# Element-wise steps of the first half moved from GpSimd to VectorE, and the first norm's gains moved from the weights into the tokens

## The chip, the core and the metric

The kernel runs on one core of a Trainium2 chip. The core has five engines that work in parallel and meet at semaphores: TensorE (PE, matrix products; PEld is its weight load), VectorE (DVE), ScalarE (ACT), GpSimd (POOL) and SyncE (SP, which here only issues transfers). Each engine takes its instructions in one fixed order. The metric is the device time of one execution in microseconds (us). Lower is better.

## The reference, cut to what matters

One decoder layer for 2048 tokens of width 1024, all in float32. Only the first half (up to the output projection) is touched by the change:

```
h     = rmsnorm(x, norm1_g)                        # gains g of 1024 channels
proj  = h @ w_in                                   # 1024 -> 3*512 (attention) + 4*512 (HGRN)
# attention: three dilated branches per head, each gives o_b and lse_b
w     = softmax(lse_1, lse_4, lse_16);  o_attn = sum_b w_b * o_b
y_attn = rmsnorm(o_attn, attn_norm_g)
# HGRN2: gated recurrence, chunk by chunk
log_f = log(lb + (1-lb)*sigmoid(f_raw));  key = (1-lb)*sigmoid(-f_raw)
o_h   = rmsnorm(hgrn2(...), hgrn_norm_g);  y_hgrn = o_h * silu(gate)
x     = x + concat(y_attn, y_hgrn) @ w_out
x     = x + hier_moe(rmsnorm(x, norm2_g))          # 32 experts, top 2: not touched
out   = rmsnorm(x, norm_f_g)
```

## The kernel before, in words

The program has three stages. The first, up to about 1150 us, computes the projections, the attention and the HGRN heads; the second the output projection and the routing; the third, from about 1400 us, streams the experts' weights.

**Splitting into halves.** The large products of the first stage run as three float16 products of a high and a low part. `x_events` normalises each 128-token tile (line 226), turns it on PE (243) and splits it on ACT and DVE (246, 247). The projection weights come in pieces of 128 columns (`w_raw`): a transfer, a multiplication by the norm's gains on GpSimd (260), the sum of squares on ACT (`w_norm`, 291), a power-of-two scale (`w_scale`, `power`), and the split on ACT and DVE (`w_split`, 287, 288). The output weights go the same way in `b_weights` (GpSimd at 897).

**Pairs.** The first stage goes through four pairs of heads. For each there are projections of values (`v_tile`, PE at 386 to 388, cleared from PSUM by ACT at 393 and DVE at 394), of queries and keys (`qk_chunk`), and of the HGRN inputs (`h_tile`, PE at 567 to 569); 48 attention blocks; and four HGRN steps of 512 tokens each (`quad_steps`).

**Attention.** A block's scores (436) get bias and row maximum on DVE (440), the scaled maximum (447), the exponential on ACT (453), a split in halves on ACT and DVE (455, 456), a transposing transfer (458), and the product with the values (471, 473). The third branch is followed by `combine`: weights of the three branches from their maxima and sums (511 to 525 on DVE, 516 on ACT), then the weighted sum. Before, branch 0 is weighted on DVE and branches 1 and 2 on GpSimd (529), which also adds these two (531); DVE adds the rest (532).

**HGRN.** `gates` makes the forget gate and the key out of the projection: exponentials and logarithms on ACT (595 to 597, 601), products on DVE (598, 609) and three on GpSimd (599, 600, 602). The cumulative sum on PE (615) waits for the gate. `outputs` ends with a product on GpSimd (707).

**What sets the order.** PE's order is written out beforehand: a planner (`Runner`) strings the steps of all streams together by estimated costs and due times (`quad_steps`, for instance, allows 14,000 ns between gates and decays). The other engines' orders come out of a scheduler that follows that list with priorities, so that they shift when work moves from one engine to another.

Of the kernel before, what the change touches and what calls it, by code (L numbers as in the profile page):

```python
# [21 lines left out]
DM = 1024  # L22
# [142 lines left out]
class Layer:  # L165
# [34 lines left out]
    def x_events(self, xp, sp):  # L200
# [13 lines left out]
        def scaled(n):  # L214
# [8 lines left out]
            return rs  # L223

        def normed(n):
            nc.vector.tensor_scalar(X[n], X[n], scaled(n), None, op0=OP.mult)

        def step(n):
            if n == 0:
                for i in range(6):  # L230
                    load(i)
                for i in range(2):
                    normed(i)
# [18 lines left out]
    def w_raw(self, col, own=True):  # L252
        nc = self.nc
        if own and self.rawpool is not None:
            raw = self.rawpool.tile([128, KT, 128], F32, name="wraw0", bufs=3)
            nc.scalar.dma_start(raw, self.aps['w_in'][0, :, col:col + 128].rearrange("(t p) c -> p t c", p=128))
        else:
            raw = self.wpool.tile([128, KT, 128], F32, name="wraw", bufs=2)
            nc.sync.dma_start(raw, self.aps['w_in'][0, :, col:col + 128].rearrange("(t p) c -> p t c", p=128))
        nc.gpsimd.tensor_tensor(raw, raw, self.g1[:, :, None].to_broadcast([128, KT, 128]), op=OP.mult)  # L260
        return raw
# [31 lines left out]
    def w_steps(self, W, col, name, first):  # L293
# [7 lines left out]
        def split():  # L301
            w = W[name]
            w['sc'] = self.w_scale(w['ssp'], 1, "sc_" + name)
            self.w_split(w['raw'], w['sc'], w['wh'], w['wl'])
        a = Step(norm, 0, first)
        return [a, Step(split, 110, [(a, 10000)])]

    def h_weight_steps(self, p, W, first):
# [9 lines left out]
        def scale():  # L318
            nc = self.nc
            sc = W['sc'] = self.w_scale(W['ssp'], 4, "sc_h")  # L320
            inv = W['inv'] = self.wsm.tile([128, 2], F32, name="hinv")
            nc.vector.tensor_scalar(inv[:, 0:1], sc[:, 1:2], 1.0 / XSC, None, op0=OP.mult)
            nc.vector.tensor_scalar(inv[:, 1:2], sc[:, 1:2], -1.0 / XSC, None, op0=OP.mult)

# [173 lines left out]
    def combine(self, p, blk, rows, D):  # L498
# [14 lines left out]
        w = sm.tile([128, 3, 2, 2], F32, name="w")  # L513
        for b in range(3):
            nc.vector.tensor_sub(w[:, b], mn, nm[b])
        nc.scalar.activation(w, w, AF.Exp)
        den = sm.tile([128, 2, 2], F32, name="den")
        t = sm.tile([128, 3, 2, 2], F32, name="dent")
        for b in range(3):
            nc.vector.tensor_mul(t[:, b], w[:, b], s[b])  # L520
        nc.vector.tensor_add(den, t[:, 0], t[:, 1])
# [5 lines left out]
        for b in range(3):  # L527
            eng = nc.vector if b == 0 else nc.gpsimd
            eng.tensor_tensor(o[b], o[b], w[:, b, :, :, None].to_broadcast([128, 2, 2, 64]), op=OP.mult)
        eng = nc.gpsimd if 1 else nc.vector  # L530
        eng.tensor_tensor(o[1], o[1], o[2], op=OP.add)
        (nc.gpsimd if 1 > 1 else nc.vector).tensor_tensor(o[0], o[0], o[1], op=OP.add)
        dst = self.mix[512 * n:512 * n + 512, 128 * p:128 * p + 128].rearrange("(i r) c -> i r c", r=4)[:, r:r + 2, :]
# [47 lines left out]
    def quad_steps(self, p, q, H, ready):  # L581
# [4 lines left out]
        def gates():  # L586
# [11 lines left out]
            nc.vector.tensor_mul(key, key, f)  # L598
            nc.gpsimd.tensor_tensor(f, f, oml, op=OP.mult)
            nc.gpsimd.tensor_tensor(f, f, lb, op=OP.add)  # L600
            nc.scalar.activation(f, f, AF.Ln)
            nc.gpsimd.tensor_tensor(key, key, oml, op=OP.mult)

# [80 lines left out]
        def outputs():  # L684
# [3 lines left out]
            for i in range(4):  # L688
# [4 lines left out]
                for h in range(2):  # L693
# [12 lines left out]
                                    rs[:, :, None].to_broadcast([128, 8, 64]), op=OP.mult)  # L706
            nc.gpsimd.tensor_tensor(y, y, hq[:, :, 128:256], op=OP.mult)
            nc.sync.dma_start(self.mix[q * 512:q * 512 + 512, 512 + 128 * p:640 + 128 * p]
# [10 lines left out]
    def phase_a(self, ctx, pairs=range(NPAIR)):  # L719
# [10 lines left out]
        with pools:  # L730
# [9 lines left out]
            self.vp = pool("vp", 2)  # L740
            self.g1 = apool.tile([128, KT], F32, name="g1")
            nc.scalar.dma_start(self.g1, self.aps['norm1_g'][0].rearrange("(t p) -> p t", p=128))
            self.Sp = apool.tile([128, 8, 128], F32, name="Sp")
# [141 lines left out]
    def b_weights(self, pool, first, free):  # L885
# [8 lines left out]
        def piece(k):  # L894
            raw = self.wpool.tile([128, KT, 128], F32, name="wraw", bufs=2).rearrange("p t c -> p (t c)")
            nc.sync.dma_start(raw, aps['w_out'][0, 128 * k:128 * k + 128, :])
            nc.gpsimd.tensor_scalar(raw, raw, gm[:, k:k + 1], 1.0, op0=OP.mult, op1=OP.mult)
            return raw

        def norm(k):  # L900
            junk = self.wpool.tile([128, KT, 128], F16, name="wl", bufs=3).rearrange("p t c -> p (t c)")
            self.w_norm(piece(k), ssp, k, junk)

        def scale():
            self.wo = self.xpool.tile([128, 2], F32, name="wo", bufs=1)
            self.w_scale(ssp, KT, self.wo)
            self.inv = self.wo[:, 1:2]

        def split(k):
            if k % 4 == 0:  # L910
                for w, i in ((self.wH, 0), (self.wL, 1)):
                    t = self.xpool.tile([128, KT, 512], F16, name=f"x{i}{k // 4}", bufs=1)
                    w += [t.rearrange("p t c -> p (t c)")[:, DM * j:DM * j + DM] for j in range(4)]
            self.w_split(piece(k), self.wo, self.wH[k], self.wL[k])
        out = [Step(lambda k=k: norm(k), 0, first) for k in range(KT)]
# [1014 lines left out]
```

## Time and profile before

| | |
|---|---|
| median of 3 runs | 2192.49 us (2183.34 to 2193.94) |
| profiled execution | 2186.48 us, span 2184.7 us |
| PE busy | 1959.5 us (90%) |
| DVE busy | 1491.8 us (68%) |
| ACT busy | 1178.6 us (54%) |
| POOL busy | 489.6 us (22%) |
| mean granted PE clock | 0.949 |

Busy times are sums over the whole span; they average over stages that differ. An instruction that an engine has begun and that is held up inside counts as busy. The granted clock is given as a share: 1 is the upper of TensorE's two levels (2.4 GHz), 0.5 the lower (1.2 GHz), and a mean in between says how long each lasted.

### The profile page before, as it was taken

The page shows a single profiled execution, that of the slowest core. Times are in us where ns is not written, and L with a number is a line of the kernel's source. Part 1 is how long each engine was busy: PE and PEld are TensorE (multiplying, and loading weights), DVE is VectorE, ACT ScalarE, POOL GpSimd, SP SyncE. Part 2 cuts the span into 40 slices and gives each one's busy share as a digit, 9 for nine tenths or more (in the row PEclk, how much of TensorE's full clock was granted, in tenths as well). Part 3 has the DMA queues.
Part 4 walks back from the last instruction along what each step waited for, and adds up shares of the span by engine and source line. Part 5 has one row for each costly group of instructions (what it writes and reads, how often), then busy time and mean ns, then how long its engine had stood idle before and what let it go on. Part 6 is the DMA issues. An engine that isn't in the chain of part 4 may idle for free. (4 is left out here: it accounts for less than half of the span.)

```text
span 2184.7 us, 39474 instructions
## 1 busy us (share of the span) xinstructions
PE 1959.5 (90%) x13777; PEld 1342.0 (61%) x13777; DVE 1491.8 (68%) x4158; ACT 1178.6 (54%) x2581; POOL 489.6 (22%) x491
## 2 busy tenths in 40 slices
PE   4998979999899998998879898899999999999981
PEld 4645566555655557455444445769999977666650
DVE  6657588767867688568776677866566666565525
ACT  6455554665547555666544343555565555454524
POOL 2302143113421125212320012122233221111110
PEclk9999989999999999999888998899999999999995
DMA  7334155533545234643468995899999999999857
GB/s 237 82 95 105 50 127 125 115 90 74 127 110 132 64 91 120 184 102 99 112 170 226 273 260 164 322 346 313 313 316 306 332 325 313 332 320 323 293 150 295
DMA packets 438895, 433.37 MB, mean 198 GB/s; under 512 B 242644, under 2 KB 325716, under 8 KB 438176
## 3 DMA queue, kind: packets, MB, share of 16 engines
q1 hardware_dynamic: 420464, 382.74, 57.6%
q0 software_dynamic: 14064, 46.46, 8.6%
q8 instruction: 109, 1.79, 0.3%
q10 hardware_dynamic: 4160, 1.58, 0.3%
q14 instruction: 98, 0.80, 0.1%
HBM read 305.30 MB, written 66.29 MB: 170 GB/s over the span
## 5 line engine op out<-in xcount | busy, mean ns | idle before, releaser
L1653 DVE TENSOR_TENSOR eL<-eraw,eH 128x1024 bf16<-128x1024 f32 x252 | 302.6, 1217 | 100.2 <-ACT eH L1646 93.3
L1646 ACT ACTIVATE eH<-eraw 128x1024 fp32r<-128x1024 f32 x252 | 258.6, 1053 | 116.5 <-PE acc L1754 48.7
L453 ACT ACTIVATE P<-S,orow,fqk 128x256 f32<-128x256 f32 (+1 forms) x384 | 194.8, 512 | 169.9 <-DVE orow L447 92.1
L567 PE MATMUL proj<-whh,x 128*128 128x512 f16 x512 | 201.9, 394 | 4.1 <-ACT hq L574 4.1
L568 PE MATMUL proj<-whl,x 128*128 128x512 f16 x512 | 200.8, 392 | 0.0
L569 PE MATMUL proj<-whh,x 128*128 128x512 f16 x512 | 200.4, 391 | 0.0
L1735 PE MATMUL acc<-xs,eH 128*128 128x352 f32 (+15 forms) x1216 | 195.2, 314 | 1.2 <-DVE xs L1712 1.2
L440 DVE CUSTOM_DVE_ANT_0 S<-S,bias 128x256 f32<-128x256 f32 (+1 forms) x384 | 141.7, 369 | 74.5 <-PE S L436 71.1
L436 PE MATMUL S<-k,qs 128*128 128x256 f16 (+1 forms) x768 | 172.0, 355 | 13.3 <-ACT P L453 10.6
L1735 PEld LDWEIGHTS acc<-xs,eH 128*128 128x128 f32 x1216 | 176.2, 191 | 4.1 <-issue 2.2
L456 DVE TENSOR_TENSOR Ps<-P,Ps 128x256 f16<-128x256 f32 (+1 forms) x192 | 128.0, 667 | 65.9 <-ACT Ps L455 64.8
L1785 PE MATMUL acc<-hs,eD 128*128 128x176 f32 (+15 forms) x1216 | 164.9, 295 | 2.7 <-DVE ts L1760 2.5
L1785 PEld LDWEIGHTS acc<-hs,eD 128*128 128x128 f32 x1216 | 161.1, 190 | 3.9 <-DVE ts L1760 3.1
L1837 POOL DMA_INDIRECT x2d<-yo,sidx x49 | 104.9, 2141 | 255.9 <-DVE yo L1812 96.8
L436 PEld LDWEIGHTS <-qs 128*128 128x128 f16 x768 | 89.1, 123 | 68.4 <-issue 18.4
L260 POOL TENSOR_TENSOR wraw<-wraw,g 128x1024 f32<-128x1024 f32 x44 | 85.1, 1936 | 205.7 <-DMA wraw<-in_w_in_dram 178.4
L1695 POOL DMA_INDIRECT xg<-h2d,gidx x49 | 53.6, 1094 | 334.8 <-PE tr L1709 161.1
L1797 PE MATMUL acc<-eD,hs 128*128 128x512 f32 x208 | 97.8, 608 | 23.5 <-ACT yo L1810 13.8
L1753 PE MATMUL acc<-eH,xs 128*128 128x512 f32 x208 | 118.5, 570 | 0.0
L386 PE MATMUL proj<-wh,x 128*128 128x128 f16 x512 | 94.2, 228 | 17.4 <-DVE V L394 17.4
L455 ACT ACTIVATE Ps<-P 128x256 f16<-128x256 f32 (+1 forms) x192 | 102.7, 535 | 7.4 <-DMA PT<-Ps 4.8
L348 PE MATMUL proj<-x,wh 128*128 128x512 f16 x256 | 98.4, 384 | 1.7 <-DVE k L359 1.7
(396 smaller groups left out, 4748.0 us busy)
## 6 DMA issues: line engine op xcount, KB each, us to landing
eraw<-in_w_up_dram SPq DMA_DIRECT2D x128, 512.0 KB, 6.2
eD<-in_w_down_dram SPq DMA_DIRECT2D x128, 512.0 KB, 6.3
eraw<-in_w_gate_dram SPq DMA_DIRECT2D x124, 512.0 KB, 7.2
wraw<-in_w_in_dram SPq DMA_DIRECT2D x41, 512.0 KB, 4.5
od<-orow SPq DMA_DIRECT2D x64, 132.0 KB, 2.1
R<-od SPq DMA_DIRECT2D x64, 132.0 KB, 2.4
xt<-in_x_dram SPq DMA_DIRECT2D x16, 512.0 KB, 4.8
wraw<-in_w_out_dram SPq DMA_DIRECT2D x16, 512.0 KB, 3.9
```

The costliest lines, as they stand in the source:

```text
L436: nc.tensor.matmul(ps[:, h, :W], q, self.block_cols(D['k'][h][:, x], br, blk, True), start=(x == 0), stop=(x == 1))
L440: nc.vector.tensor_tensor_reduce(ps[:, h, :W], ps[:, h, :W], bias[:, 256 - W:256], 1.0, -3.0e38, OP.add, OP.max, mx[:, h:h + 1])
L453: nc.scalar.activation(P[:, h], ps[:, h, :W], AF.Exp, bias=nm[:, h:h + 1], scale=f[:, h:h + 1], accum_out=orow[:, 130 + h:131 + h])
L456: nc.vector.tensor_tensor(hv[:, 1], P, hv[:, 0], op=OP.subtract)
L567: nc.tensor.matmul(ps, self.XH[n // 4][:, k, ns], W['whh'][:, k, :], start=(k == 0), stop=False)
L568: nc.tensor.matmul(ps, self.XH[n // 4][:, k, ns], W['whl'][:, k, :], start=False, stop=False)
L569: nc.tensor.matmul(ps, self.XL[n // 4][:, k, ns], W['whh'][:, k, :], start=False, stop=(k == KT - 1))
L1646: self.last_high = self.nc.scalar.activation(H, raw, AF.Copy).ins
L1653: self.last_low = self.nc.vector.tensor_sub(L, raw, H.bitcast(F32)).ins
L1735: nc.tensor.matmul(gu[:, i, 0:2 * cap], w[:, o:o + 128], xs[:, k], start=(k == 0), stop=False, skip_group_check=True)
L1753: nc.tensor.matmul(gu[:, j], xs[:, k, 0], H[:, fs], start=(k == 0), stop=False)
L1785: nc.tensor.matmul(py[:, j, 0:cap], W['w_down', f][:, o:o + 128], hs[:, f], start=(f == 0), stop=(f == 3))
```

## The change

The gains of the first norm are no longer multiplied into the weights (260 goes) but into the tokens: the tile's scaling (226) becomes an operation with two tensor inputs. For this the gains are loaded as a 128x1024 tile, and a new function `factors` finds their largest square, takes a power of two from it and scales them. That power is undone in the scales of the projections (`su_...`, `hinv`). In `gates`, `outputs` and `combine` the operations of GpSimd go to DVE. In `combine` small operations on branches 1 and 2 are joined to one, and each branch is weighted and added in turn. The gains of the output weights go into the scale of ACT's square and into the scale of the split (897 goes).

```
+        g = xp.tile([128, DM], F32, name="g1b", bufs=1)
+        nc.scalar.dma_start(g, bass.AP(tensor=src.tensor, offset=src.offset, ap=[[0, 128], [1, DM]]))
+        def factors():
+            for i, op in enumerate((OP.max, OP.min)):
+                nc.vector.tensor_reduce(m[:, i:i + 1], g, axis=AX.X, op=op)
+            nc.vector.tensor_mul(m, m, m)
+            nc.vector.tensor_max(m[:, 0:1], m[:, 0:1], m[:, 1:2])
+            self.power(m[:, 0:1], sg, sp.tile([128, 1], I32, name="ge"))
...
+            nc.vector.tensor_scalar(g, g, sg[:, 0:1], None, op0=OP.mult)
         def normed(n):
-            nc.vector.tensor_scalar(X[n], X[n], scaled(n), None, op0=OP.mult)
+            nc.vector.scalar_tensor_tensor(X[n], X[n], scaled(n), g, op0=OP.mult, op1=OP.mult)
...
-        nc.gpsimd.tensor_tensor(raw, raw, self.g1[:, :, None].to_broadcast([128, KT, 128]), op=OP.mult)
...
+            w['sc'] = self.wsm.tile([128, 2], F32, name="su_" + name)
+            nc.vector.tensor_mul(w['sc'], sc, self.sg)
...
-        for b in range(3):
-            nc.vector.tensor_sub(w[:, b], mn, nm[b])
+        nc.vector.tensor_sub(w[:, 0], mn, nm[0])
+        nc.vector.tensor_tensor(w[:, 1:3], mn[:, None].to_broadcast([128, 2, 2, 2]), R[:, :, :, 128:130], op=OP.subtract)
...
-            eng = nc.vector if b == 0 else nc.gpsimd
-            eng.tensor_tensor(o[b], o[b], w[:, b, :, :, None].to_broadcast([128, 2, 2, 64]), op=OP.mult)
-        eng = nc.gpsimd if 1 else nc.vector
-        eng.tensor_tensor(o[1], o[1], o[2], op=OP.add)
-        (nc.gpsimd if 1 > 1 else nc.vector).tensor_tensor(o[0], o[0], o[1], op=OP.add)
+            nc.vector.tensor_tensor(o[b], o[b], w[:, b, :, :, None].to_broadcast([128, 2, 2, 64]), op=OP.mult)
+            if b:
+                nc.vector.tensor_add(o[0], o[0], o[b])
...
-            nc.gpsimd.tensor_tensor(f, f, oml, op=OP.mult)
-            nc.gpsimd.tensor_tensor(f, f, lb, op=OP.add)
+            nc.vector.tensor_mul(f, f, oml)
+            nc.vector.tensor_add(f, f, lb)
             nc.scalar.activation(f, f, AF.Ln)
-            nc.gpsimd.tensor_tensor(key, key, oml, op=OP.mult)
+            nc.vector.tensor_mul(key, key, oml)
...
-            nc.gpsimd.tensor_tensor(y, y, hq[:, :, 128:256], op=OP.mult)
+            nc.vector.tensor_mul(y, y, hq[:, :, 128:256])
...
-            nc.gpsimd.tensor_scalar(raw, raw, gm[:, k:k + 1], 1.0, op0=OP.mult, op1=OP.mult)
...
-            self.w_norm(piece(k), ssp, k, junk)
+            nc.scalar.activation(junk.bitcast(BF16), piece(k), AF.Square, scale=gm[:, k:k + 1], accum_out=ssp[:, k:k + 1])
...
+            nc.vector.tensor_scalar(gm, gm, self.wo[:, 0:1], None, op0=OP.mult)
...
-            self.w_split(piece(k), self.wo, self.wH[k], self.wL[k])
+            self.w_split(piece(k), gm[:, k:k + 1], self.wH[k], self.wL[k])
```

In the kernel's order the change reads as follows at two places (line numbers of the changed kernel are 19 to 21 higher there; ISA at 440 and 461 is the bias with the maximum).

First, the gates of the second step of 512 tokens in the second pair. GpSimd's order before, with the end of the preceding step's `outputs` (`qT`) ahead of the three operations on the gate (`hq`) and the key:

```order
L707 TENSOR_TENSOR qT<-qT,hq 128x512
L599 TENSOR_TENSOR hq<-hq,lb 128x4x128
L602 TENSOR_TENSOR key<-key,lb 128x512
L600 TENSOR_TENSOR hq<-hq,lb 128x4x128
L423 TENSOR_SCALAR bias<-cta,slope 128x256
```

DVE's order before at the same gates, from the key's product on:

```order
L598 TENSOR_TENSOR key<-key,hq 128x512
L447 TENSOR_TENSOR orow<-mx,fqk 128x2
L572 TENSOR_SCALAR hq<-proj,hinv 128x384
L482 TENSOR_TENSOR orow<-O,otmp 128x2x128
L456 TENSOR_TENSOR Ps<-P,Ps 128x256
```

DVE's order now:

```order
L617 TENSOR_TENSOR key<-key,hq 128x512
L468 TENSOR_TENSOR orow<-mx,fqk 128x2
L628 TENSOR_TENSOR hq<-hq,sg 128x2x256
L503 TENSOR_TENSOR orow<-O,otmp 128x2x128
L477 TENSOR_TENSOR Ps<-P,Ps 128x256
L618 TENSOR_TENSOR hq<-hq,lb 128x4x128
L461 ISA S,mx<-S,bias 128x128
L461 ISA mx 128x1
L619 TENSOR_TENSOR hq<-hq,lb 128x4x128
```

Two of the three operations on the gate's way (618 and 619) now stand among the attention's, the last of them eight rows behind the key's product; the third (621) comes five rows later.

Second, DVE around the first clearing of the value projection (`V<-proj`) at the start of the third pair, before:

```order
L704 TENSOR_TENSOR qT<-hg,hrs 128x512
L609 TENSOR_TENSOR hq<-hq,sg 128x2x256
L598 TENSOR_TENSOR key<-key,hq 128x512
L609 TENSOR_TENSOR hq<-hq,sg 128x2x256
L394 SCALAR_TENSOR_TENSOR V<-proj,V 128x8x64
```

and now:

```order
L723 TENSOR_TENSOR qT<-hg,hrs 128x512
L726 TENSOR_TENSOR qT<-qT,hq 128x512
L628 TENSOR_TENSOR hq<-hq,sg 128x2x256
L617 TENSOR_TENSOR key<-key,hq 128x512
L628 TENSOR_TENSOR hq<-hq,sg 128x2x256
L618 TENSOR_TENSOR hq<-hq,lb 128x4x128
L621 TENSOR_TENSOR key<-key,lb 128x512
L619 TENSOR_TENSOR hq<-hq,lb 128x4x128
L415 SCALAR_TENSOR_TENSOR V<-proj,V 128x8x64
```

All four operations that came from GpSimd (726, 618, 621, 619) stand ahead of the clearing. PE's order is the same in both programs but for two products of the output projection that stand a few rows later.

## Rows read from the trace of the kernel before

**Rows 1.** Busy times by stage; x counts instructions, PEclk is the granted clock.
```profile
core 0: us, PE busy (x) PEld busy (x) DVE busy (x) ACT busy (x) POOL busy (x), PEclk, DMA share, GB/s
0.00:40.00 40.00, 12.27 (x60) 10.82 (x61) 22.62 (x81) 24.55 (x54) 10.10 (x10) 1.00 0.79 251
100.00:1000.00 900.00, 833.53 (x6070) 514.10 (x6068) 653.34 (x2194) 514.17 (x1363) 227.58 (x230) 0.96 0.43 106
1000.00:1150.00 150.00, 120.09 (x682) 67.95 (x681) 122.21 (x433) 82.98 (x217) 44.67 (x46) 0.86 0.56 139
1150.00:2184.00 1034.00, 935.90 (x6470) 709.54 (x6468) 642.69 (x1331) 519.84 (x869) 188.24 (x190) 0.95 0.90 291
```

**Rows 2.** The same view around three of PE's waits.
```profile
216.00:232.00 16.00, 11.82 (x48) 6.51 (x48) 8.92 (x27) 6.69 (x23) 4.13 (x4) 0.68 0.21 58
306.00:326.00 20.00, 8.87 (x95) 7.76 (x93) 18.05 (x45) 9.17 (x23) 13.56 (x12) 0.66 0.54 137
496.00:508.00 12.00, 9.92 (x44) 5.66 (x43) 5.54 (x22) 6.29 (x21) 2.65 (x4) 0.72 0.21 55
```

**Rows 3.** PE's waits from 100 to 1180 us: total, times, longest (us).
```profile
PE proj L386 <- DVE V L394: 17.4, 3, 11.1
PE hg L615 <- ACT hq L601: 9.4, 4, 4.2
```

**Rows 4.** POOL's groups by line, whole span: busy us, mean ns, idle before.
```profile
L260 POOL TENSOR_TENSOR wraw<-wraw,g 128x1024 f32<-128x1024 f32 x44 | 85.1, 1936 | 205.7 <-DMA wraw<-in_w_in_dram 178.4 <-ACT key L698 7.8 <-DVE Se L659 4.9
L529 POOL TENSOR_TENSOR R<-R,w 128x256 f32<-128x256 f32 x64 | 41.4, 666 | 152.5 <-DVE w L525 123.9 <-DVE mn L512 18.5 <-DVE rs_t L193 4.2
L531 POOL TENSOR_TENSOR R<-R 128x256 f32<-128x256 f32 x32 | 26.1, 815 | 2.4
L600 POOL TENSOR_TENSOR hq<-hq,lb 128x512 f32<-128x512 f32 x16 | 23.2, 1451 | 0.0
```

**Rows 5.** DVE's groups by line and shape, 0 to 1180 us.
```profile
L456 DVE TENSOR_TENSOR Ps<-P,Ps 128x512 f16<-128x512 f32 x108 | 86.9, 804 | 32.6 <-ACT Ps L455 31.8
L447 DVE TENSOR_TENSOR orow<-mx,fqk 128x2 f32<-128x2 f32 x192 | 39.9, 208 | 2.4
L609 DVE TENSOR_TENSOR hq<-hq,sg 128x512 f32<-128x512 f32 x32 | 32.7, 1038 | 2.0 <-ACT sg L606 2.0
L529 DVE TENSOR_TENSOR orow<-orow,w 128x256 f32<-128x256 f32 x32 | 14.3, 448 | 0.4
L525 DVE TENSOR_TENSOR w<-w,den 128x12 f32<-128x12 f32 x32 | 5.5, 171 | 0.4
```

**Rows 6.** DVE in order of time, 306 to 326 us: start, duration, instruction.
```profile
308.50 1.75 DVE L456 TENSOR_TENSOR Ps<-P,Ps 128x512 f16<-128x512 f32 x1
310.17 0.42 DVE L440 CUSTOM_DVE_ANT_0 S<-S,bias 128x256 f32<-128x256 f32 x1
...
313.86 1.82 DVE L522 TENSOR_TENSOR den<-den,dent 128x4 f32<-128x4 f32 x1
...
319.28 0.68 DVE L394 SCALAR_TENSOR_TENSOR V<-proj,V 128x512 f16<-128x512 f32 x1
...
321.75 0.69 DVE L456 TENSOR_TENSOR Ps<-P,Ps 128x512 f16<-128x512 f32 x1
...
325.24 0.16 DVE L522 TENSOR_TENSOR den<-den,dent 128x4 f32<-128x4 f32 x1
```

**Rows 7.** DVE in order of time, 484 to 500 us.
```profile
484.56 0.16 DVE L447 TENSOR_TENSOR orow<-mx,fqk 128x2 f32<-128x2 f32 x1
...
493.43 0.68 DVE L598 TENSOR_TENSOR key<-key,hq 128x512 f32<-128x512 f32 x1
```

**Rows 8.** DVE in order of time, at the start.
```profile
36.70 0.75 DVE L226 TENSOR_SCALAR xt<-xt,rs 128x1024 f32<-128x1024 f32 x1
37.36 1.28 DVE L288 SCALAR_TENSOR_TENSOR wl<-wraw,sc_v,wh 128x1024 f16<-128x1024 f32 x1
```

**Rows 9.** ACT in order of time, 576 to 594 us.
```profile
593.52 0.63 ACT L601 ACTIVATE hq<-hq 128x512 f32<-128x512 f32 x1 [6.17 <-POOL hq L600]
```

More of the change, by code (lines that the diff above doesn't have):

```diff
@@ L223, in scaled @@
             return rs
+        g = xp.tile([128, DM], F32, name="g1b", bufs=1)
+        src = self.aps['norm1_g'][0]
+        nc.scalar.dma_start(g, bass.AP(tensor=src.tensor, offset=src.offset, ap=[[0, 128], [1, DM]]))
+        sg = self.sg = self.apool.tile([128, 2], F32, name="sg1")
+        def factors():
+            m = sp.tile([128, 2], F32, name="gm2")
+            for i, op in enumerate((OP.max, OP.min)):
[3 more added lines that the diff above has]
+            self.power(m[:, 0:1], sg, sp.tile([128, 1], I32, name="ge"))
+            nc.vector.tensor_scalar(sg[:, 0:1], sg[:, 0:1], 2.0 ** -15, None, op0=OP.mult)
+            nc.vector.tensor_scalar(sg[:, 1:2], sg[:, 1:2], 2.0 ** 15, None, op0=OP.mult)
+            nc.vector.tensor_scalar(g, g, sg[:, 0:1], None, op0=OP.mult)
         def normed(n):
-            nc.vector.tensor_scalar(X[n], X[n], scaled(n), None, op0=OP.mult)
+            nc.vector.scalar_tensor_tensor(X[n], X[n], scaled(n), g, op0=OP.mult, op1=OP.mult)
         def step(n):
@@ L231, in step @@
                     load(i)
+                factors()
                 for i in range(2):
@@ L304, in split @@
             self.w_split(w['raw'], w['sc'], w['wh'], w['wl'])
+            nc, sc = self.nc, w['sc']
+            w['sc'] = self.wsm.tile([128, 2], F32, name="su_" + name)
+            nc.vector.tensor_mul(w['sc'], sc, self.sg)
         a = Step(norm, 0, first)
@@ L321, in scale @@
             inv = W['inv'] = self.wsm.tile([128, 2], F32, name="hinv")
-            nc.vector.tensor_scalar(inv[:, 0:1], sc[:, 1:2], 1.0 / XSC, None, op0=OP.mult)
-            nc.vector.tensor_scalar(inv[:, 1:2], sc[:, 1:2], -1.0 / XSC, None, op0=OP.mult)
+            nc.vector.tensor_scalar(inv[:, 0:1], sc[:, 1:2], self.sg[:, 1:2], 1.0 / XSC, op0=OP.mult, op1=OP.mult)
+            nc.vector.tensor_scalar(inv[:, 1:2], inv[:, 0:1], -1.0, None, op0=OP.mult)
         def split(j):
@@ L518, in combine @@
         t = sm.tile([128, 3, 2, 2], F32, name="dent")
-        for b in range(3):
-            nc.vector.tensor_mul(t[:, b], w[:, b], s[b])
+        nc.vector.tensor_mul(t[:, 0], w[:, 0], s[0])
+        nc.vector.tensor_mul(t[:, 1:3], w[:, 1:3], R[:, :, :, 130:132])
         nc.vector.tensor_add(den, t[:, 0], t[:, 1])
@@ L740, in phase_a @@
             self.vp = pool("vp", 2)
-            self.g1 = apool.tile([128, KT], F32, name="g1")
-            nc.scalar.dma_start(self.g1, self.aps['norm1_g'][0].rearrange("(t p) -> p t", p=128))
             self.Sp = apool.tile([128, 8, 128], F32, name="Sp")
```

## The prediction, made before the changed kernel was run

> **What bounds the kernel now.** I read first the busy times by stage [rows 1]. From 1150 us on the change touches nothing but the output weights' preparation, which is over by then, so those 1034 us stay. In the first stage PE is the engine that the rest serves: from 100 to 1000 us it works 833.5 of 900 us, from 1000 to 1150 us 120.1 of 150. What a change can win there is PE's idle time, 66.5 + 29.9 = 96 us, and what the lower clock costs: a mean of 0.96 over 900 us and of 0.86 over 150 is 36 + 21 = 57 us of work lost. The ceiling is 153 us. DVE is the second engine, at 73% of the 900 us and 81% of the 150.
>
> Next, the same view around PE's waits [rows 2]. From 306 to 326 us DVE is busy 18 of 20 us while PE has 8.9 and a clock of 0.66: DVE sets the pace there, for a while. PE's list of waits names the places [rows 3]: 17.4 us in three waits until DVE has cleared the value projection, 9.4 us in four until ACT has the gate.
>
> Then, DVE in order of time in the longest of them, and this decides the case [rows 6]. L522, an addition of four elements per row, takes 1.82 us at 313.86 and 0.16 at 325.24; the split L456 takes 1.75 at 308.50 and 0.69 at 321.75. Between the two long ones L440 takes its usual 0.42. L522 and L456 have two inputs in SBUF, L440 reads PSUM and one SBUF tensor, and GpSimd was multiplying tiles throughout (13.6 of the 20 us [rows 2]). So part of DVE's busy time is DVE being held by GpSimd.
>
> How much in all: by form, mean less the unheld duration, times the count [rows 5, 6, 7]. L456: 108 x (0.804 - 0.69) = 12.3 us; L609: 32 x (1.038 - 0.68, the same size in L598) = 11.5; L447: 192 x (0.208 - 0.16) = 9.2. These three make 33 us, the safe end. Done for the 32 forms, from L456 down to L525 (0.171, where nothing is left), it makes 110 us up to 1250 us.
>
> **Part by part.** Everything below is DVE time unless named, and each size comes from a row.
>
> 1. Gates and outputs: 48 + 16 operations of 128x512 at 0.68 (L598 [rows 7]) = +43.5 us.
> 2. Merges: 32 calls with three more operations of 128x256 at 0.448 (L529 [rows 5]) = +43; two small ones fewer in each, 64 x 0.16 [rows 6] = -10.
> 3. Tokens: the tile's scaling takes a second tensor. The trace has no such operation on the tokens; the nearest is L288, 1.28 against 0.75 of L226 [rows 8], so 16 x 0.53 = +8.5. It can't be below 0 (as fast as now).
> 4. `factors`: two reductions and one scaling of 1024 columns, each between 0.75 and 1.28 [rows 8], and 11 small ones at 0.16: 4 to 6 us, I take 5. They run while DVE waits for the first tokens. The `su` products: 12 x 0.16 = 2.
> 5. Removed: the holding, -33 to -110 us. I take the upper end, since all 44 weight products of 1.9 us, the merges and the gates leave GpSimd [rows 4], and only 12 bias tiles still read there.
>
> Sum on DVE: 92 - 110 = -18 us, bounds +59 and -18. By itself that is little. What counts is where: the holding comes in bursts at the waits, the new work is spread, and 0.68 us at most stand where up to 2 us of holding stood.
>
> The rule behind the row: the Trainium skill ("SBUF — State Buffer", Who interferes with whom) says that a DVE instruction with two SBUF inputs and a GpSimd instruction that reads SBUF block each other for a whole instruction. The trace agrees (1.82 against 0.16 us, L440 untouched). By that rule nearly the whole 110 us go; without it only what the three largest forms show would be sure, and the sum on DVE would be +59.
>
> PE's path, against the profiled execution of 2186.5 us:
>
> - **Waits for the gate** (9.4 us in four [rows 3]). At 496 to 508 us the clock of 0.72 costs 12 x 0.28 = 3.4 us more, at 216 to 232 us 16 x 0.32 = 5.1 [rows 2]; the third is like the first, the fourth short: 21 us in all. Now the chain after the key's product is three GpSimd operations of 1.45 [rows 4], with other GpSimd work ahead of them: 4.3 us or more. After, the order has six or seven DVE rows up to the second gate operation, 0.16 to 0.69 each, about 3 us. Each wait loses 1.3 us or more, the first over 4; what is left is too short for most of the clock's falls. Of 21 us I take -14 (bounds 0 and -21).
> - **Waits for the value projection** (17.4 us in three). The first, 11.1 us, ends at 319.28 when L394 starts. The DVE operations from L456 at 308.50 on lose about 6 us to holding before it, 2.7 of them in the two shown [rows 6]; the moved operations, 4 x 0.68, take 2.7 back. Also ACT's logarithm (L601) stood before the clearing and waited for GpSimd; in the same place of the third pair that was 6.17 us [rows 9]. I take 3 us off for DVE, 3 for ACT, and 3 of the 6.8 that the clock cost there (20 x 0.34 [rows 2]). The other two waits, 3 us each, keep their length: four moved operations (4 x 0.68) stand ahead of the clearing, about what holding they replace. -9 (bounds +3 and -20).
> - **1000 to 1150 us**: 30 us idle and 21 by the clock [rows 1]. Holding and new work there nearly balance (GpSimd is busy 45 us). A sixth: -8 (bounds +10 and -20).
> - **All other idle time up to 1000 us**: 66.5 - 27 = 40, and 36 less the 18 named (12 + 6) = 18 by the clock, 58 us. ACT and SP also queue behind GpSimd's results. Under a tenth: -5 (bounds +5 and -25).
> - **Start**: the first tiles wait now for `factors` and ACT issues a 512 KB load more; the weights no longer pass GpSimd (1.9 us each). +1 (bounds -4 and +6, twelve tiles' 0.53).
> - **New waits**: score operations that queue behind a moved operation of 0.68 us in stretches where PE is dense: +5 (bounds 0 and +15).
>
> Output weights: 16 GpSimd products go, ACT's square and split take the gains as a scale and cost what they cost; beside other work, 0.
>
> Sum: -14 - 9 - 8 - 5 + 1 + 5 = -30, so 2156.5 us. The profiled run lies 6 us under the median of 2192.5, and the three runs spread over 11 us; I put the forecast at 2158.
>
> **Rivals.**
>
> *The time goes elsewhere (no change).* DVE has as much to do as before (92 on, 110 off), PE's order is the same, and each wait that shrinks lets PE run into the next one that its order holds. For it: the second and third wait for the value projection come out even. Against it: the waits for the gate hang on GpSimd's own slow operations. With half of the gate's and of the first value wait (-11) and 5 for new waits: 2186.5 - 6 = 2180, within 2176 and 2192.
>
> *DVE becomes the bound (slower).* Place: the merges and the end of the stage, where DVE is at 80 to 90% [rows 1, 2]. It decides if the holding that goes is nearer to 33 than to 92 us. Each merge then costs DVE 3 x 0.448 - 2 x 0.16 = 1.0 us more and its share of gates 2.7 per step. In the five stretches of 50 us around the four merges and the end that is about 6 us each, 30 us, straight on PE's path, with the clock falling in longer waits: 2186.5 + 20 to 35, about 2213. The Trainium skill ("Perfetto Trace Analysis", Optimizing Scalar/DVE Operations) speaks for this side: with DVE saturated, handing work to ScalarE or even GpSimd may pay, and the change goes the other way. The same passage warns that the shared port may eat the gain, and rows 6 show that here it did.
>
> *Most of the stalls go.* Holding and queues behind GpSimd feed ACT and SP too. If the gate's and the value's waits go whole with their clock (21 + 27) and a third of the rest of the 153 us: 2186.5 - 80 = about 2105.
>
> That the change doesn't do what it says (GpSimd goes on holding DVE): 12 bias tiles and the transfers that GpSimd issues remain; too little for a case of its own.
>
> **How the numbers follow.** What a measurement here can tell from no change is about 0.5%, 11 us. The forecast (2158, own range 2140 to 2178): 0.55. Most of the stalls go: 0.17. No change: 0.18. Slower: 0.10. The range of 8 in 10 reaches down into the large gain and up through no change: 2118 to 2195. Faster by over 0.5% (under 2181.5): the forecast's 0.55, the large gain's 0.17 and a little of the third = 0.74; within 0.5%: 0.16; slower: 0.10.
>
> **What would show it.** Right: L522, L447 and L456 at their unheld 0.16, 0.16 and 0.69 us throughout; DVE's busy time in the first stage about equal; the waits of PE for the gate gone or under 1 us, with no fall of the clock behind them; the value projection's first wait about half. Wrong: long DVE operations of a few elements with GpSimd idle; more PE waits for DVE (440, 447) in the merges; a first transposed token much later than before with the whole stage shifted by it.

## The result, and the profile after

| | before | changed |
|---|---|---|
| median | 2190.47 us (2183.34 to 2193.94, 4 runs) | 2153.7 us (2153.13 to 2154.51, 4 runs) |
| ratio, with its 95% interval | | 0.9841 [0.9812, 0.987] |
| profiled execution | 2186.48 us | 2154.51 us |
| DVE busy, whole span | 1491.8 us | 1464.4 us |
| POOL busy, whole span | 489.6 us | 231.2 us |
| mean granted PE clock | 0.949 | 0.959 |

By the ratio the change makes the kernel 35 us faster; the two profiled executions lie 32 us apart. Gains of other kernels below are worked out from their ratios in the same way. The view by stage of the changed kernel, to be read beside [rows 1]:

```profile
core 0: us, PE busy (x) PEld busy (x) DVE busy (x) ACT busy (x) POOL busy (x), PEclk, DMA share, GB/s
100.00:1000.00 900.00, 849.22 (x6193) 523.83 (x6192) 650.15 (x2348) 534.84 (x1413) 33.33 (x65) 0.97 0.47 109
1000.00:1150.00 150.00, 125.84 (x768) 71.34 (x766) 120.27 (x481) 79.82 (x203) 2.50 (x27) 0.90 0.68 172
```

PE has 849 of 900 us where it had 834, and POOL is down from 228 us to 33. DVE is as busy as before although it has taken over the work. Why, its groups by line and shape show (0 to 1150 us; busy us, mean ns, idle before), to be read beside [rows 5]:

```profile
L477 DVE TENSOR_TENSOR Ps<-P,Ps 128x512 f16<-128x512 f32 x108 | 74.3, 688 | 32.0 <-ACT Ps L476 31.0
L468 DVE TENSOR_TENSOR orow<-mx,fqk 128x2 f32<-128x2 f32 x192 | 29.6, 154 | 2.0
L551 DVE TENSOR_TENSOR orow<-orow,R 128x256 f32<-128x256 f32 x64 | 26.9, 420 | 0.4
L549 DVE TENSOR_TENSOR R<-R,w 128x256 f32<-128x256 f32 x64 | 25.0, 419 | 0.4
L628 DVE TENSOR_TENSOR hq<-hq,sg 128x512 f32<-128x512 f32 x32 | 22.0, 691 | 0.2
L243 DVE SCALAR_TENSOR_TENSOR xt<-xt,rs,g1b 128x1024 f32<-128x1024 f32 x16 | 20.5, 1280 | 0.2
L618 DVE TENSOR_TENSOR hq<-hq,lb 128x512 f32<-128x512 f32 x16 | 11.0, 686 | 0.1
```

The same split (L456 before, L477 now) takes 688 ns instead of 804, the scaled maximum (L447, L468) 154 instead of 208, the gate's product (L609, L628) 691 instead of 1038. The moved operations cost about what they were priced at: 0.686 us (0.68 expected), 0.42 (0.448), 1.280 on the tokens (1.28).

From here on "held time" is DVE's time in the first 1250 us beyond the unheld duration: in each form, the operations that lie beside a GpSimd operation on a tile, less the median of the others. It was 110 us before and is 3 us now.

PE's waits from 100 to 1150 us in the changed kernel (total, times, longest), to be read beside [rows 3]:

```profile
PE proj L586 <- ACT hq L593: 22.3, 7, 6.3
PE S L457 <- ACT P L474: 9.3, 7, 2.8
PE hg L710 <- DVE Sp L683: 9.0, 7, 5.3
PE proj L407 <- DVE V L415: 6.6, 3, 2.6
PE hg L634 <- ACT hq L620: 1.1, 3, 0.4
```

The waits for the value projection fell from 17.4 to 6.6 us and those for the gate from 9.4 to 1.1. In their place stands one that was small: PE waits 22.3 us until the gates' projection has been cleared from PSUM (L586 to L588; 4.1 us in one wait before). One of the seven, as PE sees it:

```profile
527.81 0.59 PE L586 MATMUL proj<-whh,x 128*128 128x512 f16 x1 [4.56 <-ACT hq L593]
```

And DVE, in order of time, ahead of it (start, duration, instruction):

```profile
517.44 0.69 DVE L618 TENSOR_TENSOR hq<-hq,lb 128x512 f32<-128x512 f32 x1
...
518.12 0.69 DVE L621 TENSOR_TENSOR key<-key,lb 128x512 f32<-128x512 f32 x1
...
518.80 0.68 DVE L619 TENSOR_TENSOR hq<-hq,lb 128x512 f32<-128x512 f32 x1
...
525.32 0.42 DVE L549 TENSOR_TENSOR R<-R,w 128x256 f32<-128x256 f32 x1
...
525.81 0.42 DVE L551 TENSOR_TENSOR orow<-orow,R 128x256 f32<-128x256 f32 x1
526.14 0.68 DVE L628 TENSOR_TENSOR hq<-hq,sg 128x512 f32<-128x512 f32 x1
526.75 0.61 DVE L591 TENSOR_SCALAR hq<-proj,hinv 128x384 f32<-128x384 f32 x1
```

Gates (L618 to L621, L628) and a merge (L549, L551) now stand in one queue, and the clearing (L591) behind both. No operation is held any more; DVE is simply full there (busy for 4.07 of the 4.2 us from 523.2 to 527.4).

### The profile page after: what moved, and what is told of

The parts are those of the page before. It is cut to its first block, busy times and chain, and to the rows that moved or that the text cites. A ratio compares the mean times of both kernels' runs of the same rounds, so it can differ in the third digit from the quotient of the medians.

```text
span 2152.7 us, 39239 instructions
## 1 busy us (share of the span) xinstructions
PE 1944.6 (90%) x13777; PEld 1333.9 (62%) x13777; DVE 1464.4 (68%) x4280; ACT 1181.1 (55%) x2581; POOL 231.2 (11%) x271
## 5 line engine op out<-in xcount | busy, mean ns | idle before, releaser
L586 PE MATMUL proj<-whh,x 128*128 128x512 f16 x512 | 199.4, 389 | 22.3 <-ACT hq L593 22.3
L588 PE MATMUL proj<-whh,x 128*128 128x512 f16 x512 | 197.8, 386 | 0.0
L477 DVE TENSOR_TENSOR Ps<-P,Ps 128x256 f16<-128x256 f32 (+1 forms) x192 | 109.7, 571 | 52.6 <-ACT Ps L476 51.3
L1814 PE MATMUL acc<-eD,hs 128*128 128x512 f32 x208 | 101.6, 628 | 26.8 <-ACT yo L1827 17.4
L369 PE MATMUL proj<-x,wh 128*128 128x512 f16 x256 | 98.4, 384 | 1.0 <-DVE k L380 1.0
L371 PE MATMUL proj<-x,wl 128*128 128x512 f16 x256 | 98.2, 384 | 0.0
L370 PE MATMUL proj<-x,wh 128*128 128x512 f16 x256 | 98.2, 383 | 0.0
```

The costliest lines, as they stand in the source:

```text
L477: nc.vector.tensor_tensor(hv[:, 1], P, hv[:, 0], op=OP.subtract)
L586: nc.tensor.matmul(ps, self.XH[n // 4][:, k, ns], W['whh'][:, k, :], start=(k == 0), stop=False)
L588: nc.tensor.matmul(ps, self.XL[n // 4][:, k, ns], W['whh'][:, k, :], start=False, stop=(k == KT - 1))
```

## The experiments

Two theories at the outset. **H**: DVE is held inside its operations while GpSimd reads tiles, and each read that leaves GpSimd gives that back. **L**: DVE's total is no limit; what counts is that others waited for GpSimd's slow results, the gate's above all. The line numbers differ a little from kernel to kernel; the operations are the same.

### One part at a time

Each of these is the kernel before with one part of the change alone.

Gates:

```
-            nc.gpsimd.tensor_tensor(f, f, oml, op=OP.mult)
-            nc.gpsimd.tensor_tensor(f, f, lb, op=OP.add)
+            nc.vector.tensor_mul(f, f, oml)
+            nc.vector.tensor_add(f, f, lb)
...
-            nc.gpsimd.tensor_tensor(key, key, oml, op=OP.mult)
+            nc.vector.tensor_mul(key, key, oml)
```

> The kernel before with only the three gate operations (599, 600, 602) on DVE. Theory H (the gain is DVE no longer held by GpSimd reading SBUF): the gain goes with the GpSimd time that is taken away, 69 of some 285 us, so 8 to 12 us faster. Theory L (the gain is that ACT, and PE behind it, no longer wait for slow GpSimd results): this part carries most of it, 18 us or more faster, and the four waits of PE for the gate go.

Merges (with the small operations joined, as in the whole change):

```
-            eng = nc.vector if b == 0 else nc.gpsimd
-            eng.tensor_tensor(o[b], o[b], w[:, b, :, :, None].to_broadcast([128, 2, 2, 64]), op=OP.mult)
...
+            nc.vector.tensor_tensor(o[b], o[b], w[:, b, :, :, None].to_broadcast([128, 2, 2, 64]), op=OP.mult)
+            if b:
+                nc.vector.tensor_add(o[0], o[0], o[b])
```

> The kernel before with only the merges of the branches on DVE. H: 67 us of GpSimd reading go, 3 us of DVE work per call come; 5 to 10 us faster. L: nobody on PE's way waits for a merge, DVE has 33 us more to do in its densest stretches: 0 to 10 us slower.

Tokens:

```
-            nc.vector.tensor_scalar(X[n], X[n], scaled(n), None, op0=OP.mult)
+            nc.vector.scalar_tensor_tensor(X[n], X[n], scaled(n), g, op0=OP.mult, op1=OP.mult)
...
-        nc.gpsimd.tensor_tensor(raw, raw, self.g1[:, :, None].to_broadcast([128, KT, 128]), op=OP.mult)
```

> The kernel before with only the first norm's gains moved from the weights into the tokens. H: 85 us of GpSimd reading go, the largest share: 10 to 15 us faster although the start is 2 us later. L: the weights are ready long before PE needs them, so between 3 us faster and 2 us slower.

Outputs (with the output gains in the scales, as in the whole change):

```
-            nc.gpsimd.tensor_tensor(y, y, hq[:, :, 128:256], op=OP.mult)
+            nc.vector.tensor_mul(y, y, hq[:, :, 128:256])
...
-            nc.gpsimd.tensor_scalar(raw, raw, gm[:, k:k + 1], 1.0, op0=OP.mult, op1=OP.mult)
```

> The kernel before with only the product at the end of the HGRN outputs on DVE and the gains of the output weights in the scales. H: 42 us of GpSimd reading go, half of it late in the stage: 4 to 7 us faster. L: 0 to 3 us faster. If the four parts add up, they make some 35 us.

Measured (medians; ratio to the kernel before; PE's waits in us from 100 to 1150 us):

| part alone | us | ratio, 95% | held, us | wait for the gate | for V | for the clearing |
|---|---|---|---|---|---|---|
| gates | 2183.15 | 0.9963 [0.9944, 0.9983] | 78 | 4.6 | 24.0 | 17.4 |
| merges | 2193.24 | 1.0031 [1.0009, 1.0054] | 93 | 9.5 | 14.0 | none |
| tokens | 2150.62 | 0.9838 [0.9821, 0.9855] | 66 | 5.2 | 6.3 | 4.1 |
| outputs | 2170.1 | 0.9925 [0.9901, 0.9949] | 99 | 9.9 | 13.9 | none |

The gains in the tokens alone bring the whole gain of the change; the merges alone make the kernel a little slower (by 2 to 12 us, the ends of the interval), though they take 18 us of holding away. Neither theory fits all four. The gates came out as H said (8 us) and the merges as L said. The tokens and the outputs won more than either allowed: L gave them next to nothing, and H shared the gain out in proportion to the reads. The sum of the four is -8 + 7 - 35 - 16 = -52 us, and the whole brings -35: the parts do not add up.

The tokens' part takes more than one thing away, and no run tells them apart: 44 us of holding, the weight products' place in GpSimd's queue, and their place between the transfer of a weight piece and ACT. In the kernel before, ACT waited for these products (60 to 1150 us):

```profile
ACT whh L287 <- POOL wraw L260: 19.2, 6, 6.3
ACT wl L291 <- POOL wraw L260: 10.1, 3, 7.1
```

and with the tokens alone it waits for the transfer itself:

```profile
ACT whh L304 <- DMA wraw<-in_w_in_dram: 19.8, 8, 4.2
```

With the smaller groups of the same kind that is 32 us before and 23 with the tokens alone, so that 9 us of this waiting go beside 44 us of holding; how the 35 us divide between the causes stays open. Why the outputs alone win as much as 16 us stays open as well. SyncE's transfer queue is one candidate: its waits for that product fell from 39.5 us in 15 waits to 19.6 in ten. Another is seen at PE's second and third wait for the gate: they last 1.74 us instead of 2.08 and 2.09, and the granted clock from 492 to 504 us and from 744 to 758 is 1.00, where it was 0.72 and 0.76 around the same waits before. With the merges alone these waits kept their length, and the clock around them was 1.00 and 0.88; so what such a wait costs in clock is not fixed.

One reason why the parts do not add up is seen in the kernel with the gates alone:

```profile
PE proj L386 <- DVE V L394: 24.0, 3, 8.6
PE proj L567 <- ACT hq L574: 17.4, 4, 6.0
```

Moving the gates halves the wait for the gate, and at once brings the wait for the clearing up from 4.1 to 17.4 us, with GpSimd's weight products still there. So this new wait comes with the gates, not with the rest. The waits for the value projection grow too, from 17.4 to 24.0 us.

### GpSimd's reads put back, and a control

In the changed kernel, GpSimd gets reads again at the places of the removed work, into a scratch tile that nobody uses.

```
+        for i in range(2):
+            nc.gpsimd.tensor_tensor(self.scr, self.scr, raw.rearrange("p t c -> p (t c)")[:, 512 * i:512 * i + 480], op=OP.add)
...
+        for b in range(3):
+            nc.gpsimd.tensor_tensor(s4, s4, w[:, b, :, :, None].to_broadcast([128, 2, 2, 64]), op=OP.add)
...
+            for _ in range(4):
+                nc.gpsimd.tensor_tensor(s4, s4, hq[:, 0:3, 384:512], op=OP.add)
```

> The changed kernel, in which GpSimd again reads SBUF at the places of the removed work: two additions of 128x480 from each weight tile, four of 128x384 in each step of the gates, one in each of the outputs, three of 128x256 in each merge, all into a scratch tile that nobody reads. Nothing waits for GpSimd's sums, so only its use of the memory is put back, not its place in any chain. Theory H (DVE is held while GpSimd reads): DVE's operations get longer again by 70 to 110 us in sum up to 1150 us, PE's waits for DVE come back, and the time rises by 15 to 40 us over the changed kernel's 2153.7, to 2169 to 2194. Theory Q (what counted was that ACT, DVE and PE had GpSimd's results to wait for): DVE's operations may get longer, but the time stays within 5 us of the changed kernel's.

The control has at the same places copies of one column and fills (here the weights'):

```
+        nc.gpsimd.tensor_copy(self.scr[:, 0:1], raw[:, 0, 0:1])
+        for i in range(2):
+            nc.gpsimd.memset(self.scr, 1.0)
...
```

> The control for the kernel that reads: at the same places of the changed kernel GpSimd copies one column of the same tile (so that the same buffers have one more reader) and then fills the scratch tile, without reading a tile at length. Theory H: with no two-input reads on GpSimd, DVE's operations stay as in the changed kernel (lengthened by under 20 us in sum) and the time is 2150 to 2160. Theory Q and the view that any work of GpSimd costs (its queue, the buffers' later release) say the same time as with the reads.

With the reads: 2230.69 us, 1.0181 [1.0155, 1.0207]. With the fills: 2151.25 us, 0.983 [0.9808, 0.9852], the same as the changed kernel. GpSimd's groups in the kernel with the reads (0 to 1180 us):

```profile
L279 POOL TENSOR_TENSOR scr<-scr,wraw 128x480 f32<-128x480 f32 x88 | 120.1, 1365 | 176.6 <-DMA wraw<-in_w_in_dram 171.6
L630 POOL TENSOR_TENSOR scr<-scr,hq 128x384 f32<-128x384 f32 x64 | 70.0, 1094 | 150.7 <-ACT hq L598 146.5
L552 POOL TENSOR_TENSOR scr<-scr,w 128x256 f32<-128x256 f32 x96 | 68.2, 710 | 219.1 <-DVE w L548 162.5 <-DVE w L538 23.5 <-DVE mn L535 12.8
```

DVE's groups in the same kernel (0 to 1150 us):

```profile
L479 DVE TENSOR_TENSOR Ps<-P,Ps 128x512 f16<-128x512 f32 x106 | 78.6, 742 | 30.3 <-ACT Ps L478 29.3
L554 DVE TENSOR_TENSOR R<-R,w 128x256 f32<-128x256 f32 x60 | 39.6, 688 | 0.3
L470 DVE TENSOR_TENSOR orow<-mx,fqk 128x2 f32<-128x2 f32 x191 | 39.5, 207 | 2.0
```

And with the fills:

```profile
L480 DVE TENSOR_TENSOR Ps<-P,Ps 128x512 f16<-128x512 f32 x108 | 74.6, 690 | 32.5 <-ACT Ps L479 31.4
L555 DVE TENSOR_TENSOR R<-R,w 128x256 f32<-128x256 f32 x64 | 25.0, 418 | 0.3
L471 DVE TENSOR_TENSOR orow<-mx,fqk 128x2 f32<-128x2 f32 x192 | 29.6, 154 | 2.0
```

The scaled maximum is back at 207 ns (208 before the change) with the reads and at 154 with the fills; the merge's product goes from 418 to 688. Held time is 117 us against 4. So reads hold DVE and fills hardly do, and 113 us more of held DVE time cost 79 us. Theory H is shown in kind; in size it missed, since it had expected 15 to 40 us. Theory Q, as the whole cause, falls: in the trace with the reads no engine's wait for its work up to 1150 us ends with one of GpSimd's sums, and the transfer queue's do so in four places, 3 us in all. Nor is it the weight tiles' later release, although a read takes 1.37 us and a fill 0.50: from 60 to 1150 us ACT waits 26 us for the weights' transfers with the reads and 25 with the fills. Only up to 118 us, where the score products start 12 us later than with the fills (PE works 74.3 us there against 84.3), are the two causes not told apart. PE's waits with the reads:

```profile
PE proj L591 <- ACT hq L598: 29.2, 7, 7.0
PE hg L718 <- DVE Sp L691: 18.9, 4, 7.8
PE proj L409 <- DVE V L417: 18.6, 3, 6.4
```

The wait for the value projection is back at 18.6 us (17.4 before, 6.6 without the reads). The kernel is slower than before the change; that this is because DVE now has the moved work and the holding at once is argued, not tried.

### Twice the gates' moved work on DVE

Four additions more in each step of the gates, again into the scratch tile:

```
+            for _ in range(4):
+                nc.vector.tensor_add(s4, s4, hq[:, 0:3, 384:512])
```

> The changed kernel with four more additions of 128x384 on DVE in each of the 16 steps of the gates, 64 x about 0.5 = 32 us of DVE work up to 1150 us. Theory H: spread work on DVE is paid only where PE waits for DVE; a third to a half is paid, 2160 to 2172. The view that DVE had slack after the change: within 4 us of 2153.7. The view that DVE is the bound of this stage: all of it, 2180 to 2190.

2160.05 us, 0.9852 [0.982, 0.9885]; beside the changed kernel's 0.9841 [0.9812, 0.987] the intervals overlap. The additions took 35 us of DVE (64 of 0.55 us), and this spread work cost between nothing and some 15 us. That DVE is the bound of the stage is excluded; between the other two views this run does not decide.

### The clearing earlier in its queues

```
+            with self.tc.high_priority(offset=130):
+                nc.vector.tensor_scalar(H['hq', q][:, i, 0:384], ps[:, 0:384], W['inv'][:, 0:1], -80.0, op0=OP.mult,
+                                        op1=OP.max)
+                nc.scalar.activation(H['hq', q][:, i, 384:512], ps[:, 384:512], AF.Copy, scale=W['inv'][:, 0:1])
```

> The changed kernel in which the two instructions that clear the gates' projection from PSUM (one on DVE, one on ACT) are put earlier in their queues, ahead of the merges and gates that the scheduler has placed before them. In the changed kernel PE waits 22.3 us in seven waits for this clearing. Theory A (these waits are a matter of order in the queues): they go to under 8 us and the time falls by 6 to 15 us, to 2139 to 2148. Theory B (DVE is full in these stretches, and what is put back comes to be waited for): PE's waits move to other tiles and the time stays within 4 us of 2153.7.

2163.95 us, 0.9872 [0.9845, 0.9899]: no gain, rather a loss. The 22.3 us of waits are gone from the list; what heads it now:

```profile
PE S L457 <- ACT P L474: 10.6, 5, 2.8
PE hg L711 <- DVE Sp L684: 8.0, 9, 3.4
PE hg L690 <- DVE dS L674: 6.9, 4, 2.2
PE hg L671 <- DVE brs L194: 5.9, 1, 5.9
```

and the stages:

```profile
100.00:1000.00 900.00, 851.73 (x6158) 523.96 (x6156) 640.93 (x2324) 528.52 (x1396) 35.17 (x66) 0.96 0.46 107
1000.00:1150.00 150.00, 129.06 (x738) 73.77 (x737) 123.54 (x481) 84.32 (x214) 1.95 (x21) 0.87 0.67 164
```

PE is busy a little longer than in the changed kernel (851.7 against 849.2 us, 129.1 against 125.8), but at a lower clock (0.96 and 0.87 against 0.97 and 0.90), and it has done fewer products in that time (6158 and 738 against 6193 and 768). Theory A falls: the wait was a matter of order in the queue, but putting it away only moved it. A wait's length in the list is not what its removal is worth.

### Toward a better version

The kernel before with two or three of the parts; the edits are those shown above. Without the merges:

> The whole change but for the merges, which stay as before: GpSimd does four of the five operations on 128x256 of each merge. Beside the changed kernel this takes some 43 us of additions and products off DVE and puts GpSimd's reads of the merges back, which are worth about 18 us of holding (what the merges alone took away). Theory M (the merges were the one part that cost: alone they made the kernel before 7 us slower): 3 to 10 us faster than the changed kernel's 2153.7, so 2144 to 2151. Theory H in its plain form (every read of GpSimd that goes is a gain): 3 to 10 us slower, 2157 to 2164.

The tokens and the outputs alone:

> The kernel before with two parts of the change alone, those that won most by themselves: the gains into the tokens (-35 us alone) and the outputs' product with the output gains in the scales (-16 alone). Gates and merges stay on GpSimd. If the two gains add up: 2135 to 2142. If the tokens' part already takes all that PE's waits have to give: 2147 to 2153, as the tokens alone (2150.6).

The tokens and the gates alone:

> The kernel before with the gains into the tokens and the gates on DVE; the outputs and the merges stay on GpSimd. If the gains add up (-35 and -8 alone): 2143 to 2148. If the weight products alone were what held the gates back, so that moving the gates as well adds only DVE work: 2149 to 2156.

And, once these three were known, all but the gates:

> The whole change but for the gates, whose three operations on 128x512 stay on GpSimd. In the four kernels so far that have them on DVE, PE waits 17 to 22 us for the gates' projection to be cleared; in those that have them on GpSimd, 0 to 4 us. Theory G (it is the gates on DVE that stand ahead of that clearing, and that cost makes the whole change worth less than its parts): these waits go to under 6 us here, and the time is 2135 to 2147, faster than the whole change's 2153.7. Theory M (the merges on DVE stand ahead of it as well, or cost as much by themselves): the waits stay over 10 us or move to other places, and the time is 2150 to 2160.

| moved | us | ratio, 95% | held, us | wait for the clearing | for dS (hg) |
|---|---|---|---|---|---|
| all four | 2153.7 | 0.9841 [0.9812, 0.987] | 3 | 22.3 | 0.6 |
| tokens, outputs, gates | 2158.95 | 0.9855 [0.9827, 0.9883] | 20 | 20.3 | 3.6 |
| tokens, gates | 2151.97 | 0.9827 [0.9804, 0.985] | 36 | 17.8 | 6.3 |
| tokens, outputs, merges | 2146.52 | 0.9795 [0.9765, 0.9824] | 38 | none | 14.7 |
| tokens, outputs | 2138.75 | 0.9763 [0.9734, 0.9792] | 53 | none | 9.2 |

The best version moves only the tokens' gains and the outputs, and leaves gates and merges on GpSimd: 2138.75 us, 52 us faster than before, and its interval lies below that of the whole change (that of the kernel without the gates overlaps it). There the two parts' gains add up (-35 and -16). Tokens and gates do not add up: 2151.97 us is no faster than the tokens alone. Both together bring the wait for the gate to 1.5 us, but the wait for the clearing comes in its place. In the kernel without the merges theory M fell: it is no faster than the whole. Its 2158.95 us lies where H in its plain form put it, but the intervals overlap, and the best version, which keeps 53 us of holding, speaks against that form.

Theory G held: with the gates on DVE the wait for the clearing is 17 to 22 us in each of these kernels (9.6 with the doubled gates, where PE waits 15.4 us for the state instead), with the gates on GpSimd at most 4.1. Without the gates the change does better by 7 us in the medians and 10 by the ratios, though the two intervals still touch. The merges leave their mark in another place. In the kernel without the gates:

```profile
PE hg L689 <- DVE dS L673: 14.7, 4, 5.1
PE S L457 <- ACT P L474: 11.1, 7, 2.8
PE hg L634 <- ACT hq L620: 5.2, 3, 1.7
```

PE waits for the state's update (dS), as it did with the merges alone (15.0 us in four waits, 6.8 in two before). With both merges and gates on DVE that wait is 0.6 us, presumably because PE already stands at the clearing. The best version has no long wait left:

```profile
PE S L457 <- ACT P L474: 10.2, 6, 2.8
PE hg L691 <- DVE dS L675: 9.2, 5, 3.5
PE hg L636 <- ACT hq L622: 5.2, 3, 1.7
```

Its stages, the first with more PE time than in the whole change (849 us) and a higher clock (0.97 there):

```profile
100.00:1000.00 900.00, 854.93 (x6279) 526.72 (x6277) 655.06 (x2325) 540.75 (x1433) 142.35 (x180) 0.98 0.48 112
1000.00:1150.00 150.00, 127.88 (x781) 70.30 (x779) 119.72 (x466) 78.49 (x203) 28.66 (x57) 0.91 0.74 181
```

And this with GpSimd's gates still at work, and DVE's scaled maximum still held (196 ns on average):

```profile
L620 POOL TENSOR_TENSOR hq<-hq,lb 128x512 f32<-128x512 f32 x16 | 23.2, 1450 | 326.9 <-DVE key L619 326.9
```

So held time by itself does not rank the kernels (53 us in the best, 3 in the whole change). The reading that fits is that its cost depends on whether PE waits for DVE at that place: 22 of the 44 weight products came in three bursts (295 to 355, 576 to 622 and 832 to 868 us), at the projections of the values, where it does. No run put the reads of the weights back alone.

## Why the prediction was right

2158 us were predicted and 2153.7 measured. That GpSimd's reads hold DVE, and that this costs time, is the mechanism that it named, and the runs with reads and with fills show it. How much of the change's own gain is holding, and how much is that ACT no longer waits for GpSimd's results, no run tells apart. The terms that missed did so with opposite signs, so that the total comes this close is in part luck. Measured at the same score product in both profiled traces (how much earlier it starts in the changed kernel), term by term:

- **Start, +1**: the score products near 118 us start 1.6 us later, at 163 us they are even. Right; in seven other kernels with this start they come 1.5 to 4.7 us later near 118 us. ACT waits 8.38 us there for its first weight tile; whether the load that was added delays that transfer was not tried.

```profile
16.67 1.06 ACT L308 ACTIVATE wl<-wraw 128x1024 bf16<-128x1024 f32 x1 [8.38 <-DMA wraw<-in_w_in_dram]
```

- **Waits for the gate, -14**: around the first three the lead grows by 5.4 (214 to 225 us), 4.8 (470 to 507) and 4.8 (751 to 763): -15. Right; the idle time went nearly whole. As for the cause, the three GpSimd operations of the gate were half of it. The gates alone bring the wait to 4.6 us and leave most of the first one (3.1 of 4.2 us). The tokens alone bring it to 5.2 and take just the first one, where a weight product (212.33 us) and the end of `outputs` stood ahead of the gate in GpSimd's queue. Both together bring it to 1.5.
- **Waits for the value projection, -9, and new waits, +5**: the two can't be read apart by time, since the new wait at 523 us (4.56 us) and the one at 773 (4.56) stand in the same stretches. Together, from 225 to 278, 278 to 375, 524 to 633 and 780 to 893 us, the lead falls by 1.2 and grows by 3.4, 0.1 and 0.7: -3, where -4 was expected. By the list of waits both terms were mis-sized: the value's waits lost 10.8 of 17.4 us idle, with their clock more (the first went from 11.1 to 2.6 us, where about half was expected), and the new waits are 22.3 instead of 5 us. In that first wait before, DVE was busy without a break from 306.4 to 319.3 us, and an estimate from the unheld durations makes 7.7 us of this holding. The step that failed is the one on new waits: it looked for them at the score operations, where the moved operations are short beside a dense PE, and not at the next thing in DVE's queue that PE can't do without, the clearing of the projection.
- **1000 to 1150 us, -8**: from 981 to 1150 us the lead grows from 27.3 to 37.4: -10, although two of the new waits (4.4 and 6.3 us) stand there. From there to the experts' first product it grows to 40.2, another -3 where nothing was expected.
- **All other idle time, -5**: what is left of the lead at 981 us is 9, so -9. More than half of it, 5.1, comes from 163 to 214 us, where PE's wait for the state went from 3.6 to 1.1 us.
- **Experts, 0**: from their first product to their last the lead falls from 40.2 to 34.1 us; nothing there was changed. In the kernel with the tokens alone it falls by 5.1, with tokens and outputs by 1.4. That it is the streaming of the weights that takes this back was not tried.

DVE's sum: -18 predicted, -27 measured over the whole span (1491.8 to 1464.4). The upper end of the holding, 110 us, was the right one: 107 of it went. "Unheld 0.16, 0.16 and 0.69 throughout" came out as 0.156 (the addition of four elements), 0.154 and 0.688.

Of the rivals, "the time goes elsewhere" had a share in it: with the gates on DVE, PE runs into the clearing, and the whole change gave back some 15 us that tokens and outputs alone keep. "DVE becomes the bound" is excluded by the doubled gate work; its place, the merges, was right in so far as the merges cost some 7 us when they move alone. "Most of the stalls go" did not come; the best version goes a third of the way from the forecast to it. What the prediction lacked was the parts: it credited the gain to all moves alike, while one of them, the weight products, alone wins as much as the whole, and two of them, gates and merges, are worth nothing or less once it is made.

## What to carry to other kernels

When small two-input operations of DVE take ten times their usual time beside a working GpSimd, look for GpSimd's long reads of SBUF where PE waits for DVE, and take those away first, best by folding the work into an operation that runs anyway (here the gains into the tokens' scaling). Work that GpSimd does where PE is dense may stay: here, moved to DVE, it stood in the queue ahead of something that PE needs. Move one part at a time and time the combinations; the parts' gains added up only for tokens and outputs.

## What was not expected of the hardware

GpSimd's fills hardly hold DVE: some 106 us of them (88 of 128x480 and 96 of 128x256 among them) and 57 us of one-column copies left 4 us of held time, where 278 us of two-input reads made 117. Nor are operations of DVE that read PSUM held: the bias with the maximum at 128x256 took a mean of 424 ns in the 30 cases that lay beside GpSimd's reads, and a median of 426 in the 186 others. The Trainium skill ("SBUF — State Buffer", Who interferes with whom) states both, for GpSimd instructions that only write (against DVE instructions with two SBUF inputs), and for DVE instructions with at most one SBUF input outside the modes that use two ports; the traces agree.

One SBUF input alone is no safe sign, though. In the kernel with the fills a copy of one tensor on DVE (median 0.29 us) lasted as long as a fill:

```profile
591.12 0.67 DVE L692 COPY Sp<-dS 64x256 f32<-64x256 f32 x1
590.99 0.66 POOL L737 MEMSET scr<- 128x480 f32 x1
```

And in the kernel before, beside GpSimd's products, the tokens' scaling by one number per row (L226) once took 2.27 us instead of 0.75, the copy L664 once 1.12 instead of 0.29, and the scaling of four elements (L524) up to 2.45 instead of 0.22. Which mode these instructions ran in no run here shows.
